# Attention scores on one core: the second score product over all 128 rows, with zeros in place of the other head

## The chip, the cores and the metric

The kernel runs on one core of a Trainium2 chip. Its engines have queues of their own and meet only at semaphores: TensorE (PE, with the weight loads shown apart as PEld), VectorE (DVE), ScalarE (ACT), GpSimd (POOL) and SyncE (SP, which issues most DMAs). The metric is device time of one execution in microseconds (us), lower is better.

## The reference, cut to what matters

Two kinds of transformer block follow each other, two layers of each, on 512 tokens of width 1024. Both have an attention with heads of 64 features. In the first kind it is grouped: eight query heads share two key heads, and every token sees every other.

```python
proj = rms_norm(x, attn_norm_g[i]) @ w_in[i]
q, k, v, u, vv = jnp.split(proj, split_at, axis=-1)
q = axial_rope(rms_norm(q.reshape(b, s, N_HEADS, HEAD_DIM), q_norm_g[i]), tables)
k = axial_rope(rms_norm(k.reshape(b, s, N_KV_HEADS, HEAD_DIM), k_norm_g[i]), tables)
attn_o = gqa_attention(q, k, v)
```

In the second kind the attention is causal and dilated, with four heads, beside a convolution and a gated delta rule. All is float32, and the feed-forward halves of the blocks hold most of the products.

## The kernel before, in words

Activations lie feature-major: 128 features on the partitions, 512 tokens along the free axis. Products run in float32r, which holds fewer bits, so an operand is split into a high and a low part, and a dense product is made of three: high by high, high by low and low by high (`mm3`, L307 to L309).

A chunk of the attention holds two heads of 64 features, one on partitions 0 to 63 and one on 64 to 127 (`UP`, `DN`). For the scores the three products are folded into two. `stack_q` makes one tile a head: the high part of the query on the head's own partitions and its low part on the other 64. `stack_k` makes one tile a head with the high part of the key on both halves, so that one product over 128 rows gives high by high plus low by high. The third term, high by low, is a second product into the same PSUM tile. Its operands are the head's own 64 rows of the query tile and of a tile with the low parts of both heads (`kl` in the first kind of block, `akl` in the second).

A unit is 128 queries of one chunk, both heads: two pairs of products (L654 and L655, in the second kind of block L1285 and L1286), for each head the row maximum (DVE, L657), the exponential with its sum (ACT, L659), then a transposition of the result by four products (L547), a copy out of PSUM (ACT for one head, L668, DVE for the other, L670), and the products with the values (L676). There are 16 units in a layer of the first kind, with 512 keys each. A layer of the second kind has 8 units, with 256, 256, 384 and 512 keys (L1288 to L1313 are their later steps).

`Driver` sets the order of the instructions once, when the program is written. It keeps a clock of assumed durations, and puts the short chains (the units among them) in front of a background of dense products. On the chip each engine works through its queue in that order and waits where an operand is late. Two units may be in flight (`st.flight < 2`), so their score products often stand together, eight in a row, with the transpositions behind them.

Squares for the norms go through a ring of two buffers called `nsq` (pool `K.np`), in `Norm.feed`, `Post.add` and once in `consts2`. POOL sums them up (L525) and later makes the reciprocal root (L453).

Of the kernel before, what the change touches and what calls it, by code (L numbers as in the profile page):

```python
# [9 lines left out]
F32 = mybir.dt.float32  # L10
# [3 lines left out]
ALU = mybir.AluOpType  # L14
# [11 lines left out]

# columns of the per-feature parameter array
C1 = {}
# [29 lines left out]

# ---- order of emission: a foreground of short chains over a background of dense products
class Driver:  # L60
# [93 lines left out]
def tl(K, tag, bufs, dt=F32, n=512, pool=None):  # L154
    """working tile of the phase's pool"""
    return (pool or K.pool).tile([128, n], dt, tag=tag, bufs=bufs, name=_nm(K, tag))


def x_slot(K, k, nm="x"):
    """the slot of a residual chunk; the residual itself waits in DRAM while others use it"""  # L160
    return K.xp.tile([128, 512], F32, tag=f"x{k}", name=_nm(K, nm))
# [37 lines left out]

# ---- weights: one stream for the whole kernel, loaded ahead, split into two exact float32r parts  # L200
IN1 = [10, 6, 11, 7, 12, 8, 13, 9, 4, 5, 0, 1, 2, 3]
AQ, AK, AV, CV, CG, GQ, GK, GV, GG = 0, 2, 4, 6, 8, 10, 14, 18, 22
# projections of the second block in the order they are made: delta rule (two heads), convolution, attention, gate
ORDER2 = ("d0", "c0", "c1", "d1", "a0", "g0", "g1", "a1", "g2", "g3")


# mixed chunks in the order they are ready
KORDER2 = (2, 3, 4, 5, 6, 7, 0, 1)
# [55 lines left out]
def w_ahead(K, upto, fine=False):  # L264
    """loads and splits up to (not with) number upto, as far as there is room"""
    nc = K.nc
# [52 lines left out]
def thin_job(K, src, H, post):  # L319
    """32 output rows: both parts of the weights in one stationary operand, their rows summed later"""  # L320
    def g():
        ps = ps_d(K)
        w, _ = next_w(K, src)
        parts = job_parts(H)
        for p in parts:
            for k in range(KD):
                wk = w[:, k * 64:k * 64 + 64]
                K.nc.tensor.matmul(ps[:64, p], wk, H.hi[k][:, p], start=(k == 0), stop=False)
                K.nc.tensor.matmul(ps[:64, p], wk, H.lo[k][:, p], start=False, stop=(k == KD - 1))
                if k == 1:  # L330
                    w_ahead(K, K.wpos + 1)
                yield 2 * MM / len(parts)
        done_w(K)
        post(ps[:64, :])

    K.drv.job(g())
# [39 lines left out]
def last_pair(K, src, xh, xl, order, post):  # L376
    """output chunks 6 and 7; the last products go by halves of the tokens, so that what waits for
    one half runs beside the products of the other"""
    n = len(order)
# [31 lines left out]
def split_into(K, hi, lo, src, act=True):  # L411
    """exact hi + lo parts of a float32 tile"""
    nc = K.nc
    if act:
        nc.scalar.copy(out=hi, in_=src)
    else:
        nc.gpsimd.tensor_scalar(hi, src, 1.0, 0.0, ALU.mult, ALU.add)
    nc.vector.tensor_tensor(lo, src, hi.bitcast(F32), ALU.subtract)
# [5 lines left out]
def stack_q(K, sa, sb, src):  # L424
    """query operands of two heads: the high part on a head's own partitions, the low part on the others"""
    nc = K.nc
# [3 lines left out]


def stack_k(K, ka, kb, lo, src):
    """key operands of two heads: the high part on both halves, the low part on a head's own partitions"""
    nc = K.nc
    for s, own, other in ((ka, UP, DN), (kb, DN, UP)):
        nc.scalar.copy(out=s[own, :], in_=src[own, :])
        nc.scalar.copy(out=s[other, :], in_=src[own, :])
        nc.vector.tensor_tensor(lo[own, :], src[own, :], s[own, :].bitcast(F32), ALU.subtract)


def tok_sums(K, acc, n=4, tag="ts"):
    """[128 tok, n] sums over the features (of each half, for n = 8)"""
    v = tiny(K, n, tag)
# [13 lines left out]
def bcast_cols(K, r, sb=None):  # L457
    """[128 tok, 4] columns -> [128, 512], the same row on every partition"""
    nc = K.nc
# [9 lines left out]
def half_rsqrt(K, acc, hv, scale, tag):  # L469
    """sums over features and their scaled rsqrt for half of the tokens, the same row on every partition"""  # L470
    nc = K.nc
# [12 lines left out]
class Norm:  # L484
    """rms norm: the gain goes into the split operand, 1/rms is left for the products"""

# [7 lines left out]
    def feed_half(self, k, x, hv, sq):  # L494
        """one half of the tokens"""
        K, nc = self.K, self.K.nc
# [46 lines left out]
def tok_transpose(K, src):  # L543
    """feature-major [128 d, 512 t] -> psum [128 tok, 4, 128 d]"""
    ps = ps_m(K)
# [13 lines left out]
def block1_mix(K, i, H, F):  # L559
# [21 lines left out]
    st.attn_done = 0  # L581
    st.flight = 0

    def qk_post(gcol, extra, then):
        """head norm over sqrt(extra) and rotation; 1/rms of the token is folded into that of the head"""
        def post(ps):
# [28 lines left out]
    def k_then(rot):  # L615
        kk, lo = (tl(K, "ka", 1, F32R), tl(K, "kb", 1, F32R)), tl(K, "kl", 1, F32R)
        stack_k(K, *kk, lo, rot)

        def start():
            st.k = (kk, lo)  # L620
        return start
# [14 lines left out]
    def attn_chunk(c):  # L636
        def then(rot):
# [7 lines left out]
            def unit(qb):  # L645
                yield lambda: st.k is not None and st.v is not None and st.flight < 2
                st.flight += 1
                kk, klo = st.k
                qs = slice(qb * 128, (qb + 1) * 128)
                ps_ = []  # L650
                for j in range(2):
                    rows = slice(64 * j, 64 * j + 64)
                    ps = ps_m(K)
                    nc.tensor.matmul(ps, qq[j][:, qs], kk[j], start=True, stop=False)  # L654
                    nc.tensor.matmul(ps, qq[j][rows, qs], klo[rows, :], start=False, stop=True)  # L655
                    nm = tiny(K, 1, "nm")
# [221 lines left out]
def tanh_silu2(K, th, y):  # L878
    """2 * silu(y)"""
    nc = K.nc  # L880
# [4 lines left out]
def block2_mix(K, i, H):  # L885
# [19 lines left out]

    # ---- decay and write strength, one column a (block, head)
    nc.scalar.activation(out=K.ea[i], in_=K.adt[i][:, 0:4], func=AF.Exp)
# [4 lines left out]
    def ab_post(ps):  # L912
# [3 lines left out]
        def g():  # L916
# [14 lines left out]
            nc.vector.tensor_scalar(beta, beta, 0.5, 0.5, ALU.mult, ALU.add)  # L931
            # softplus(x) = max(x, 0) + log1p(e), e = exp(-|x|), log1p(e) = 2 atanh(e / (2 + e))
            nc.vector.tensor_scalar(na, ad, -1.0, None, ALU.mult)
# [52 lines left out]
    class Half:  # L986
        """two heads of the delta rule"""

# [79 lines left out]

        # within a chunk: A = q k^T o decay, T = (1 + M)^-1 by doubling the solved block size
        def intra(self, b):  # L1070
# [68 lines left out]

        # across chunks  # L1140
        def rec(self):
# [62 lines left out]
        def out(self, h):  # L1204
            """gate, back to feature-major, split"""
            m = 4 + 2 * self.hp + h
# [25 lines left out]

    # ---- dilated attention: the three patterns share one maximum, keys weighted by their count
    class Attn:
# [6 lines left out]
        def qk_post(self, which):  # L1241
            def post(ps):
# [8 lines left out]
                else:  # L1251
                    lo = tl(K, "akl", 1, F32R)
                    stack_k(K, *two, lo, a)
                    self.k = two, lo
            return post
# [18 lines left out]
        def unit(self, qb):  # L1274
            qq, (kk, klo) = self.q, self.k
            n = (qb + 1) * 128
# [5 lines left out]
            for j in range(2):  # L1282
                rows = slice(64 * j, 64 * j + 64)
                ps = ps_m(K)
                nc.tensor.matmul(ps[:, :nn], qq[j][:, qs], kk[j][:, :nn], start=True, stop=False)  # L1285
                nc.tensor.matmul(ps[:, :nn], qq[j][rows, qs], klo[rows, :nn], start=False, stop=True)  # L1286
                s = tl(K, "sc", 3)
# [46 lines left out]

    # ---- conformer convolution
    st.cg = [None, None]
# [129 lines left out]
class Post:  # L1466
    """x += rms_norm(y) * gain, then the next norm, by halves of the tokens"""

# [93 lines left out]
def build(ctx, tc, A, out, n1=2, n2=2):  # L1562
# [19 lines left out]
    def consts2():  # L1582
        """what only the second block needs"""
        msk = K.const.tile([128, 5, 128], U8, tag="msk", name="msk")
# [91 lines left out]
def _consts():  # L1676
    """arrays that depend on shapes alone"""
    f = np.float32
# [36 lines left out]
def _tiles(w):  # L1715
    """[L, K, N] -> [L, N / 128, 128, K] : for each 128 columns, k chunks side by side"""
    L, Kd, N = w.shape
# [4 lines left out]
def _cols(v):  # L1722
    """[L, n * 128] -> [L, 128, n]"""
    L = v.shape[0]
    return v.reshape(L, -1, 128).transpose(0, 2, 1)


def prepare(I):
    A = _consts()
    I = {k: np.asarray(v) for k, v in I.items()}  # L1730
    A["xT"] = np.ascontiguousarray(I["x"][0].T.reshape(8, 128, 512).transpose(1, 0, 2).reshape(128, 4096))
    # chunk c of the attention holds heads c and c + 4, which use key heads 0 and 1
    hp = np.concatenate([np.arange(64) + 64 * h for c in range(4) for h in (c, c + 4)])
# [49 lines left out]
```

## Time and profile before

| | |
|---|---|
| median of three runs | 2633.65 us (2633.11, 2633.65, 2636.53) |
| profiled execution | span 2636.6 us; the time shown that stands beside it is 2636.53, so next to nothing lies around the span |
| PE busy | 2560.8 us, 97% of the span, 12988 products |
| weight loads (PEld) | 2068.5 us, 78% |
| DVE, ACT, POOL busy | 1538.3 us (58%), 1032.3 us (39%), 516.8 us (20%) |
| granted TensorE clock, mean | 0.992 of full speed |

A record of PE covers its product from the start of its stream to the modelled end, and records overlap. The distance from one start to the next is therefore what a product costs. A load record shows when the stationary operand of the product was brought into the array. "<-issue" behind an idle time means that the profile shows nothing that the engine waited for.

### The profile page before, as it was taken

Reading aid. Unit: us, or ns where it says so; the run is one execution under the profiler, and the core shown is the slowest. Engines: PE = TensorE matmul, PEld = TensorE weight load, DVE = VectorE, ACT = ScalarE, POOL = GpSimd, SP = SyncE. Lnnn points to the kernel's source line nnn. Section 1 sums busy time; section 2 is a strip of 40 time slices with the busy share of each in tenths; the row PEclk is TensorE's granted clock in tenths of the full one; section 3 lists DMA queues with packets and bytes.
Section 4 is the critical chain, followed back from the end, with each engine's and each line's share of the span. In section 5 each row is a group of like instructions: output and inputs, shape, how many; then the busy total and the mean of one; then the engine's idle time right before and its main releaser. Section 6 shows DMA issues by size and latency. Waiting matters only on the chain. (4 is left out here: it accounts for less than half of the span.)

```text
span 2636.6 us, 33494 instructions
## 1 busy us (share of the span) xinstructions
PE 2560.8 (97%) x12988; PEld 2068.5 (78%) x12988; DVE 1538.3 (58%) x2380; ACT 1032.3 (39%) x1715; POOL 516.8 (20%) x457
## 2 busy tenths in 40 slices
PE   8999999999999999999999999999889999999998
PEld 6777888878777888877777888888877777888887
DVE  6667666336766666246897554432578875644323
ACT  5554433224544433234345442222343445422221
POOL 3322111002232111003120131110221310311101
PEclk9999999999999999999999999999999999999999
DMA  4113232332113323331111322333221113232232
GB/s 162 37 33 105 96 96 95 96 109 78 33 57 100 96 96 97 112 98 41 57 41 57 96 84 100 97 92 96 87 72 37 45 42 95 85 99 96 94 94 76
DMA packets 69854, 216.05 MB, mean 82 GB/s; under 512 B 8256, under 2 KB 11968, under 8 KB 69696
## 3 DMA queue, kind: packets, MB, share of 16 engines
q1 hardware_dynamic: 68336, 212.40, 25.3%
q8 instruction: 102, 1.67, 0.3%
q10 hardware_dynamic: 1360, 1.52, 0.2%
q14 instruction: 56, 0.46, 0.1%
HBM read 207.60 MB, written 6.29 MB: 81 GB/s over the span
## 5 line engine op out<-in xcount | busy, mean ns | idle before, releaser
L307 PE MATMUL pd<-hh,wh 128*128 128x512 f32 (+1 forms) x2064 | 801.1, 392 | 12.0 <-ACT wh L285 7.8
L308 PE MATMUL pd<-hl,wh 128*128 128x512 f32 (+1 forms) x2064 | 802.2, 390 | 6.7 <-DVE hl L517 4.1
L309 PE MATMUL pd<-hh,wl 128*128 128x512 f32 (+1 forms) x2064 | 797.1, 388 | 0.9 <-DVE wl L286 0.9
L285 ACT CAST wh<-wr 128x1024 fp32r<-128x1024 f32 (+2 forms) x407 | 400.8, 986 | 985.4 <-PE pd L308 942.8
L286 DVE TENSOR_TENSOR wl<-wr,wh 128x1024 fp32r<-128x1024 f32 (+2 forms) x407 | 472.8, 1163 | 403.7 <-ACT wh L285 388.9
L307 PEld LDWEIGHTS pd<-hh,wh 128*128 128x128 f32 x2064 | 388.1, 189 | 88.1 <-ACT wh L285 7.8
L308 PEld LDWEIGHTS pd<-hl,wh 128*128 128x128 f32 x2064 | 390.8, 189 | 83.6 <-DVE hl L517 7.2
L309 PEld LDWEIGHTS pd<-hh,wl 128*128 128x128 f32 x2064 | 389.7, 189 | 75.0 <-DVE wl L286 2.0
L309 PE MATMUL pd<-gh,wl 128*128 128x512 f32 (+1 forms) x704 | 269.0, 382 | 0.0
L308 PE MATMUL pd<-gl,wh 128*128 128x512 f32 (+1 forms) x704 | 269.0, 382 | 0.0
L307 PE MATMUL pd<-gh,wh 128*128 128x512 f32 (+1 forms) x704 | 268.9, 382 | 0.0
L308 PEld LDWEIGHTS pd<-gl,wh 128*128 128x128 f32 x704 | 132.6, 188 | 28.3
L309 PEld LDWEIGHTS pd<-gh,wl 128*128 128x128 f32 x704 | 132.6, 188 | 28.3
L307 PEld LDWEIGHTS pd<-gh,wh 128*128 128x128 f32 x704 | 132.6, 188 | 28.3
L1542 POOL TENSOR_TENSOR fz<-fz,nrB 128x512 f32<-128x512 f32 x44 | 77.6, 1763 | 365.6 <-ACT fz L1541 365.6
L856 POOL TENSOR_TENSOR fy<-fy,fy 128x512 f32<-128x512 f32 x44 | 56.8, 1290 | 383.1 <-DVE fy L850 367.4
L1549 DVE TENSOR_TENSOR fz<-pd,fz 128x512 f32<-128x512 f32 x42 | 29.1, 692 | 138.3 <-PE pd L309 135.4
L846 DVE TENSOR_TENSOR fh<-pd,nrB 128x512 f32<-128x512 f32 x88 | 60.5, 688 | 59.7 <-PE pd L309 54.7
L525 POOL TENSOR_TENSOR nacc<-nacc,nsq 128x512 f32<-128x512 f32 x30 | 46.2, 1541 | 240.3 <-ACT nsq L524 239.8
L1360 DVE SCALAR_TENSOR_TENSOR cz<-cy,dwh,cz 128x501 f32<-128x501 f32 (+21 forms) x120 | 89.3, 753 | 1.2 <-ACT cz L1358 0.3
L1540 DVE TENSOR_TENSOR fz<-pd,nrB 128x512 f32<-128x512 f32 x42 | 28.9, 691 | 102.6 <-PE pd L309 102.6
L848 ACT ACTIVATE fy<-fh,cols 128x512 f32<-128x512 f32 x88 | 71.9, 817 | 36.2 <-DVE fh L846 36.2
(399 smaller groups left out, 3551.4 us busy)
## 6 DMA issues: line engine op xcount, KB each, us to landing
wr<-in_w_up_dram SPq DMA_DIRECT2D x132, 512.0 KB, 3.4
wr<-in_w_in_dram SPq DMA_DIRECT2D x80, 512.0 KB, 3.3
wr<-in_w_down_dram SPq DMA_DIRECT2D x64, 512.0 KB, 3.5
wr<-in_w_gate_dram SPq DMA_DIRECT2D x44, 512.0 KB, 3.3
wr<-in_w_down_dram SPq DMA_DIRECT2D x32, 384.0 KB, 3.1
wr<-in_w_o_dram SPq DMA_DIRECT2D x32, 256.0 KB, 2.8
wr<-in_w_out_dram SPq DMA_DIRECT2D x16, 512.0 KB, 3.3
xd<-x SPq DMA_DIRECT2D x16, 256.0 KB, 2.0
```

The source lines that it names most:

```text
L285: nc.scalar.copy(out=hi[:, cs], in_=raw[:, cs])
L286: nc.vector.tensor_tensor(lo[:, cs], raw[:, cs], hi[:, cs].bitcast(F32), ALU.subtract)
L307: nc.tensor.matmul(ps, wh, xhi, start=start, stop=False)
L308: nc.tensor.matmul(ps, wh, xlo, start=False, stop=False)
L309: nc.tensor.matmul(ps, wl, xhi, start=False, stop=stop)
L525: (nc.vector if last else nc.gpsimd).tensor_tensor(self.acc, self.acc, sq, ALU.add)
L846: nc.vector.tensor_tensor(h, ps, F.rB, ALU.mult)
L848: nc.scalar.activation(out=y, in_=h, func=AF.Identity, scale=col("cw1", tt), bias=col("cb", tt))
L856: nc.gpsimd.tensor_tensor(y, y, part.pop(t), ALU.mult)
L1360: nc.vector.scalar_tensor_tensor(zt[:, s:], y[:, :S - s], w(30 - s), zt[:, s:], ALU.mult, ALU.add)
L1542: nc.gpsimd.tensor_tensor(z, z, F.rB, ALU.mult)
L1549: nc.vector.tensor_tensor(z, ps, z, ALU.mult)
```

## The change

Each head gets a low tile of its own, taken from the `nsq` ring when the mixer of a layer begins. POOL writes zeros to the 64 partitions of the other head (two memsets a layer), and `stack_k` puts the low part on the head's own 64. The second product then takes the whole query tile and the whole low tile: the extra rows multiply the low part of the query by zero. The number of columns stays. The tiles `kl` and `akl` are gone. Lines behind it move by some 8.

```diff
+def low_keys(K):
+    lo = tl(K, "nsq", 2, F32R, pool=K.np), tl(K, "nsq", 2, F32R, pool=K.np)
+    for t, other in zip(lo, (DN, UP)):
+        K.nc.gpsimd.memset(t[other, :].bitcast(F32), 0.0)
+    return lo
...
-    for s, own, other in ((ka, UP, DN), (kb, DN, UP)):
+    for s, l, own, other in ((ka, lo[0], UP, DN), (kb, lo[1], DN, UP)):
...
-        nc.vector.tensor_tensor(lo[own, :], src[own, :], s[own, :].bitcast(F32), ALU.subtract)
+        nc.vector.tensor_tensor(l[own, :], src[own, :], s[own, :].bitcast(F32), ALU.subtract)
...
-                    nc.tensor.matmul(ps, qq[j][rows, qs], klo[rows, :], start=False, stop=True)
+                    nc.tensor.matmul(ps, qq[j][:, qs], klo[j], start=False, stop=True)
...
-                nc.tensor.matmul(ps[:, :nn], qq[j][rows, qs], klo[rows, :nn], start=False, stop=True)
+                nc.tensor.matmul(ps[:, :nn], qq[j][:, qs], klo[j][:, :nn], start=False, stop=True)
```

TensorE's queue keeps its order throughout. At the start of the first attention it stands like this before (`ka` and `kb` are the high key tiles of the two heads, `qa` and `qb` the query tiles, `pm` the scores):

```order
L654 MATMUL pm_914<-ka_728,qa_891 128x512
L655 MATMUL pm_914<-kl_730,qa_891 128x512
L307 MATMUL pd_853<-hh_175,wh_795 128x512
L654 MATMUL pm_921<-kb_729,qb_892 128x512
L655 MATMUL pm_921<-kl_730,qb_892 128x512
```

and now like this, with two tiles of the `nsq` ring in place of `kl`, every row at its old place:

```order
L662 MATMUL pm_917<-ka_732,qa_894 128x512
L663 MATMUL pm_917<-nsq_224,qa_894 128x512
L307 MATMUL pd_856<-hh_175,wh_798 128x512
L662 MATMUL pm_924<-kb_733,qb_895 128x512
L663 MATMUL pm_924<-nsq_225,qb_895 128x512
```

Only POOL's queue gets more rows. At the start of the first layer, between the last sums of the input's norm and its reciprocal root (`normr`), it held:

```order
L525 TENSOR_TENSOR nacc_117<-nacc_117,nsq_158 128x512
L525 TENSOR_TENSOR nacc_117<-nacc_117,nsq_165 128x512
L525 TENSOR_TENSOR nacc_117<-nacc_117,nsq_172 128x512
L453 TENSOR_TENSOR normr_213<-normv_211,cst 128x4
L453 TENSOR_TENSOR vvr_316<-vvv_314,cst 128x8
```

and now holds:

```order
L533 TENSOR_TENSOR nacc_117<-nacc_117,nsq_158 128x512
L533 TENSOR_TENSOR nacc_117<-nacc_117,nsq_165 128x512
L533 TENSOR_TENSOR nacc_117<-nacc_117,nsq_172 128x512
L436 MEMSET nsq_224 64x512
L436 MEMSET nsq_225 64x512
L461 TENSOR_TENSOR normr_213<-normv_211,cst 128x4
L461 TENSOR_TENSOR vvr_320<-vvv_318,cst 128x8
```

The two memsets stand ahead of the reciprocal root, and the second and third layers look the same. In the fourth they stand among the sums of a norm that is made by halves of the tokens:

```order
L461 TENSOR_TENSOR postr_15121<-postv_15119,cst 128x2
L436 MEMSET nsq_15361 64x512
L518 TENSOR_TENSOR nacc_15199<-nacc_15199,py_14481 128x256
L436 MEMSET nsq_15362 64x512
L518 TENSOR_TENSOR nacc_15199<-nacc_15199,py_14571 128x256
L461 TENSOR_TENSOR postr_15178<-postv_15176,cst 128x2
```

Without the two memset rows this is the order before.

## Rows read from the trace of the kernel before

**Rows 1.** Windows over one attention stage of each kind, busy us (instructions), granted clock

```profile
95.00:190.00 95.00, 94.06 (x605) 66.41 (x604) 63.17 (x105) 54.91 (x128) 21.83 (x20) 0.96 0.07 22
...
1395.00:1465.00 70.00, 69.28 (x381) 49.69 (x379) 52.10 (x105) 37.81 (x90) 5.50 (x5) 0.98 0.20 62
```

**Rows 2.** Waits of PE from 95 to 190 us: total, times, longest

```profile
PE pm L654 <- DVE qb L429: 0.9, 1, 0.9
```

**Rows 3.** Timeline of PE, two dense products: start, duration

```profile
97.17 0.39 PE L308 MATMUL pd<-hl,wh 128*128 128x512 f32 x1
97.40 0.40 PE L309 MATMUL pd<-hh,wl 128*128 128x512 f32 x1
```

**Rows 4.** Timeline of the weight loads, the load for the second of these

```profile
97.18 0.19 PEld L309 LDWEIGHTS pd<-hh,wl 128*128 128x128 f32 x1
```

**Rows 5.** Timeline of PE, score products of a unit, then transpositions

```profile
148.47 0.51 PE L654 MATMUL pm<-ka,qa 128*128 128x512 f32 x1
148.91 0.49 PE L655 MATMUL pm<-kl,qa 64*128 64x512 f32 x1
149.33 0.50 PE L654 MATMUL pm<-kb,qb 128*128 128x512 f32 x1
...
150.18 0.66 PE L547 MATMUL pm<-cst,tmp 128*128 128x128 f32 x4
...
152.28 1.09 PE L547 MATMUL pm<-cst,p 128*128 128x128 f32 x8
```

**Rows 6.** Timeline of the weight loads there, with idle time before

```profile
149.33 0.19 PEld L654 LDWEIGHTS pm<-kb,qb 128*128 128x128 f32 x1 [0.24 <-issue]
```

**Rows 7.** Lines L655 and L1286: count, duration in ns, first and last start, shapes

```profile
L655 PE MATMUL pm<-kl,qa x32: 491/500/792, 98.0 to 751.3; 64*128 64x512 f32 x32
...
L1286 PE MATMUL pm<-akl,aqa x16: 380/410/502, 1398.6 to 2194.6; 64*128 64x256 f32 x8, 64*128 64x384 f32 x4, 64*128 64x512 f32 x4
```

**Rows 8.** Timeline of PE, score products of the second kind of block

```profile
1441.30 0.38 PE L1286 MATMUL pm<-akl,aqa 64*128 64x256 f32 x1
1441.61 0.38 PE L1285 MATMUL pm<-akb,aqb 128*128 128x256 f32 x1
```

**Rows 9.** Timeline of PE, dense products of 256 columns

```profile
1880.94 0.28 PE L307 MATMUL pd<-gh,wh 128*128 128x256 f32 x1
1881.05 0.28 PE L308 MATMUL pd<-gl,wh 128*128 128x256 f32 x1
1881.17 0.28 PE L309 MATMUL pd<-gh,wl 128*128 128x256 f32 x1
```

**Rows 10.** Timeline of PE, a burst: first product, next work, last transposition

```profile
158.36 0.49 PE L654 MATMUL pm<-ka,qa 128*128 128x512 f32 x1
...
161.80 0.51 PE L308 MATMUL pd<-ml,wh 128*128 128x512 f32 x1
...
164.15 0.60 PE L547 MATMUL pm<-cst,p 128*128 128x128 f32 x4
```

**Rows 11.** Timeline of ACT, the first and the last exponential of that burst

```profile
160.05 0.69 ACT L659 ACTIVATE p<-pm,nm 128x512 f32<-128x512 f32 x1 [1.32 <-DVE nm L657]
...
162.71 0.69 ACT L659 ACTIVATE p<-pm,nm 128x512 f32<-128x512 f32 x1
```

**Rows 12.** Timeline of ACT, exponentials of the burst at 148.47

```profile
151.07 0.69 ACT L659 ACTIVATE p<-pm,nm 128x512 f32<-128x512 f32 x1
...
154.92 0.69 ACT L659 ACTIVATE p<-pm,nm 128x512 f32<-128x512 f32 x1
```

**Rows 13.** Windows of low clock inside attention stages, first and last of five

```profile
100.95:107.78 6.83, 6.83 (x19) 4.63 (x19) 3.78 (x6) 3.03 (x10) 0.10 (x1) 0.50 0.05 17
...
1401.43:1404.85 3.42, 3.42 (x13) 2.11 (x12) 1.72 (x5) 0.60 (x2) 0.00 (x0) 0.50 0.00 0
```

**Rows 14.** Timeline of POOL, reciprocal root of the first layer, idle before

```profile
26.04 1.03 POOL L453 TENSOR_TENSOR normr<-normv,cst 128x4 f32<-128x4 f32 x1 [6.66 <-DVE normv L451]
```

**Rows 15.** Groups of POOL by line: count, busy us, mean ns

```profile
L417 POOL TENSOR_SCALAR gh<-fy 128x512 fp32r<-128x512 f32 x44 | 29.1, 661 | 3.9
```

More of the change, by code (lines that the diff above doesn't have):

```diff
@@ L582, in block1_mix @@
     st.flight = 0
+    klo = low_keys(K)
     def qk_post(gcol, extra, then):
@@ L615, in k_then @@
     def k_then(rot):
-        kk, lo = (tl(K, "ka", 1, F32R), tl(K, "kb", 1, F32R)), tl(K, "kl", 1, F32R)
-        stack_k(K, *kk, lo, rot)
+        kk = tl(K, "ka", 1, F32R), tl(K, "kb", 1, F32R)
+        stack_k(K, *kk, klo, rot)
         def start():
-            st.k = (kk, lo)
+            st.k = kk
         return start
@@ L647, in unit @@
                 st.flight += 1
-                kk, klo = st.k
+                kk = st.k
                 qs = slice(qb * 128, (qb + 1) * 128)
@@ L651, in unit @@
                 for j in range(2):
-                    rows = slice(64 * j, 64 * j + 64)
                     ps = ps_m(K)
                     nc.tensor.matmul(ps, qq[j][:, qs], kk[j], start=True, stop=False)
-                    nc.tensor.matmul(ps, qq[j][rows, qs], klo[rows, :], start=False, stop=True)
+                    nc.tensor.matmul(ps, qq[j][:, qs], klo[j], start=False, stop=True)
                     nm = tiny(K, 1, "nm")
@@ L1231, in g_post @@
         return post
+    klo = low_keys(K)
     class Attn:
@@ L1251, in post @@
                 else:
-                    lo = tl(K, "akl", 1, F32R)
-                    stack_k(K, *two, lo, a)
-                    self.k = two, lo
+                    stack_k(K, *two, klo, a)
+                    self.k = two
             return post
@@ L1274, in unit @@
         def unit(self, qb):
-            qq, (kk, klo) = self.q, self.k
+            qq, kk = self.q, self.k
             n = (qb + 1) * 128
@@ L1282, in unit @@
             for j in range(2):
-                rows = slice(64 * j, 64 * j + 64)
                 ps = ps_m(K)
                 nc.tensor.matmul(ps[:, :nn], qq[j][:, qs], kk[j][:, :nn], start=True, stop=False)
-                nc.tensor.matmul(ps[:, :nn], qq[j][rows, qs], klo[rows, :nn], start=False, stop=True)
+                nc.tensor.matmul(ps[:, :nn], qq[j][:, qs], klo[j][:, :nn], start=False, stop=True)
                 s = tl(K, "sc", 3)
```

## The prediction

> **What bounds the kernel now.** I read first the windows over the stages that the change touches, one attention of each kind [rows 1]; the other layer of each kind looks alike. PE is busy for 94.06 of 95 us in the one and 69.28 of 70 us in the other, DVE for 63.17 and 52.10, ACT for 54.91 and 37.81. So PE's queue sets the pace. The view of waits then says what PE waits for in the first: one operand, for 0.9 us [rows 2]. Time that PE gives up there shortens the kernel until another engine's result is late.
>
> But a busy PE is not a fast one, and the third view, the timeline, shows it. Two dense products of 512 columns start 0.23 us apart [rows 3], and the load for the second begins at 97.18, just behind the start of the first at 97.17: it lies under the stream [rows 4]. Among the score products the starts are 0.44 and 0.42 us apart, and the step out to the transpositions is as long (two products fill 149.33 to 150.18, 0.85 us) [rows 5]. The load there begins with its own product, after 0.24 us idle that no semaphore explains [rows 6]. What differs is the rows: the product before it runs over 64 rows, its neighbours over 128. Each passage from 128 rows to 64 or back costs about 0.43 in place of 0.23.
>
> **What the change does to PE.** It makes the second products 128 rows tall. A 64-row product of 512 columns has a record of 0.49 us, the 128-row one beside it 0.50 or 0.51 [rows 5], so columns set the stream, and twice the rows cost nothing. What goes is the passage: one into and one out of each second product.
>
> First kind of block: 32 second products for one head [rows 7] and 32 for the other, 128 passages of 0.43 - 0.23 = 0.20 us: 25.6 us. Second kind: 16 and 16 [rows 7], 64 passages. At 256 columns the passage takes 0.31 us [rows 8] where dense products stand 0.11 and 0.12 apart [rows 9], so 0.19 each: 12.2 us (the wider ones are taken alike). Gross 37.8 us.
>
> The load of a 128-row operand behind a 128-row score product is not in the trace in just this place. Its bounds are the dense step of 0.23 and the present 0.43. I take 0.23: in shape, type and columns the new product is the same as a dense one.
>
> The first section on packing (The mechanism) in the Trainium skill's page "TensorE: Matmul & The Clock Gate" says that a weight load overlaps products in flight only when its row group differs, or when it goes to a background buffer. By the first half of that rule a full-height load would wait wherever the one before is full-height, and the change would give 0 instead of 37.8 us. The dense rows, with a full-height load under a full-height stream, do not agree with that half.
>
> **What is given back.** The order is fixed, so the gain lasts only while the exponentials keep up. Score products mostly come in bursts of eight, 1.6 us shorter each by the count above. Two bursts show what they meet.
>
> The burst from 158.36 takes until 161.80, and its last transposition starts at 164.15 [rows 10], 5.79 us after the start. By PE alone it would start after 4.19. The four exponentials start at 160.05 to 162.71 [rows 11], 0.89 apart on average, 0.69 long. Their pace is ACT's: it equals that of the present pairs of products (0.86), and won't follow products at 0.46. The first moves up by one passage to 1.49 after the start, the last then ends near 1.49 + 3 x 0.89 + 0.69 = 4.85. The transposition comes there in place of 5.79: 0.94 of 1.6 us is kept.
>
> The burst from 148.47 is tighter. The second exponential ends at 151.07 + 0.69 = 151.76 [rows 12] and its transpositions start at 152.28 [rows 5], 0.5 us later. These are followed on ACT by the copy of their result and the next two exponentials, so they hold up the rest. Here about 0.5 of 1.6 us is kept.
>
> The two together keep 45% (1.46 of 3.2), and 25.6 becomes 11.5 us. The bounds: 30% (7.7) and all (25.6). For the second kind I have no such pair; its first exponentials work on fewer columns, so I take a value between 45% and all, 70%: 8.5 us, with bounds 5.5 and 12.2.
>
> **The clock.** In the attention stages PE's clock is granted at 0.50, the lower level of 1.2 GHz, in five stretches, the first 6.83 us, the last and the three between 3.4 us each [rows 13], 20.5 us together. Work that runs there at half speed loses half the time, 10.2 us. Ahead of them stood score products with their idle passages, at times together with a wait. With denser products I expect most of these stretches to go, and take three quarters of the loss, 7.7 us, between nothing and 10.2.
>
> **What costs nothing.** Eight memsets of 64x512 on POOL. The trace has no such memset. The nearest row is an element-wise pass over 128x512 at 0.66 us [rows 15]; from nothing to 0.66 each. In the first layer POOL idles 6.66 us ahead of the reciprocal root [rows 14], which waits for DVE. The second memset has to wait for the last reader of its buffer, but that is a sum on which the root depends as well, with transpositions, a DVE reduction and a small DVE instruction between. So the memsets lie under that chain. The second and third layers have the same order. In the fourth, the memsets stand between sums that wait for ACT. Were all this cover gone, eight times 0.66 is 5.3 us. The subtractions on DVE are as many as before, into two tiles. The `nsq` ring is next needed by sums of a later phase, which need the attention's output and so come after the last score product anyway. The DMA queues are untouched.
>
> **The sum.** 11.5 + 8.5 + 7.7 - 0 = 27.7 us. The profiled execution's 2636.6 us would become 2608.9. The median lies 3 us below it. If those runs have fewer low stretches, there is less clock to regain, which argues for a little less; but the 70% may be low. I take 27.7 off the median: 2606 us, 1.1% faster.
>
> **Rivals.** *Nothing is given back*: all 37.8 us and most of the 10.2 us, below 2596. For it: PE waits for one operand only in the stage [rows 2]. Against it: the margins of 0.5 us above. 6%.
>
> *ACT takes nearly everything*: less than 30% of the first kind and 45% of the second remain, and no clock, so 5.4 to 14 us, 2619 to 2628. For it: the present pace of 0.86 us for a pair is just that of the exponentials. Against it: ACT is busy for only 54.91 of 95 us [rows 1], so between bursts it catches up. 8%.
>
> *The change doesn't do what it says*: the passage is a matter of an accumulating second product rather than of its rows, and the new ones start 0.43 apart as before. The time stays at 2634. For it: every 64-row product here is also an accumulating one. Against it: L308 and L309 accumulate as well, at 0.23. 3%. The half rule on loads named above would give the same time, and shares this chance.
>
> *Slower, by the clock*: waits for exponentials leave PE idle in short pieces at each burst, and the clock falls to 0.50 for much of the attention. Each microsecond there loses half, so 55 us more at 1.2 GHz eat the whole 27.7, and 66 us make it 2639, slower by over 0.2%; the stages of [rows 1] and their like have 330 us. For it: the clock does fall in this stage [rows 13]. Against it: it now stays at 0.96 to 0.98 on average [rows 1] although every passage leaves PE half idle, and the new waits are fewer than the passages that go. 3%.
>
> **How the numbers follow.** The forecast has 80%. Its ends: 13.2 us gained (7.7 + 5.5, no clock) is 2620; 37.8 us, everything kept and no clock, is 2596. The range 2596 to 2620 leaves out the first rival, most of the second and the last two, some 18%. A measurement of this kernel can tell about 0.2%, 5.3 us, from no change. Faster by more than that: 80 + 6 + 8 = 94%; within: 3%; slower: 3%.
>
> **What would show it.** In the profile after: score products 0.23 us apart with their loads begun under the stream before; new waits of PE for the exponential (L659 before) at transpositions, 8 to 16 us in all; fewer low stretches in the attention stages; the stages 95 to 190 and its fellow shorter by some 8 to 10 us each, those of the second kind by 4 to 6; nothing else moved. I am wrong if the products stay at 0.43, if waits take over 25 us, or if POOL's root comes late.

## The result

The changed kernel takes 2601.6 us (2599.1 to 2604.1, four runs) against 2633.4 us before in the same session: the ratio is 0.9878, 95% interval 0.9866 to 0.9890. That is 31.8 us or 1.2% faster, inside the range of 2596 to 2620 and 4 us below the forecast of 2606.

The two profiled executions differ by more, 2636.6 against 2602.3 us of span. About 1.8 us lie around the span of the changed kernel (2604.12 for 2602.3). So the profiled execution before was probably slower than the three times shown for it, and not, as was read ahead of the prediction, the one of 2636.53.

### The profile page after: what moved, and what is told of

It reads as the page before. It is cut to its first block, busy times and chain, and to the rows that moved or that the text cites. A ratio compares the mean times of both kernels' runs of the same rounds, so it can differ in the third digit from the quotient of the medians.

```text
span 2602.3 us, 33506 instructions
## 1 busy us (share of the span) xinstructions
PE 2523.3 (97%) x12988; PEld 2061.3 (79%) x12988; DVE 1535.7 (59%) x2380; ACT 1027.9 (39%) x1715; POOL 518.0 (20%) x465
```

## The profile after

The windows over one attention stage of each kind answer to [rows 1]. The stages end 12 and 30 us earlier (the last product with the values starts at 174.9 in place of 186.6, and at 1433.3 in place of 1463.7; the 30 hold what the layers ahead had gained). The windows are drawn around them and are 10 and 4 us shorter; the stages themselves lost 12.1 and 6.7 us (table below). PE's clock is now granted in full in both:

```profile
95.00:180.00 85.00, 82.58 (x613) 65.57 (x612) 63.29 (x106) 54.30 (x129) 23.82 (x22) 1.00 0.08 28
...
1375.00:1441.00 66.00, 65.27 (x383) 50.12 (x382) 53.07 (x105) 39.32 (x91) 5.48 (x5) 1.00 0.22 72
```

The timeline of PE over the burst that began at 158.36 before [rows 10] (start, duration). Products stand 0.23 us apart after the first, whichever of the two they are, and the last transposition starts 4.39 us after the first product (154.93 - 150.54), 5.79 before:

```profile
150.54 0.50 PE L662 MATMUL pm<-ka,qa 128*128 128x512 f32 x1
150.87 0.39 PE L663 MATMUL pm<-nsq,qa 128*128 128x512 f32 x1
151.10 0.40 PE L662 MATMUL pm<-kb,qb 128*128 128x512 f32 x1
151.34 0.39 PE L663 MATMUL pm<-nsq,qb 128*128 128x512 f32 x1
...
154.93 0.60 PE L555 MATMUL pm<-cst,p 128*128 128x128 f32 x4
```

At 256 columns, in the second kind of block, the step is 0.12 us:

```profile
1374.80 0.28 PE L1294 MATMUL pm<-nsq,aqa 128*128 128x256 f32 x1
1374.92 0.28 PE L1293 MATMUL pm<-akb,aqb 128*128 128x256 f32 x1
```

The weight loads of the same stretch answer to [rows 6]. The load for the third product begins at 150.88, under the stream of the second. Farther on a load waits for an exponential:

```profile
150.88 0.19 PEld L662 LDWEIGHTS pm<-kb,qb 128*128 128x128 f32 x1
...
154.19 0.42 PEld L555 LDWEIGHTS pm<-cst,p 128*128 128x128 f32 x4 [0.21 <-ACT p L667]
```

The idle time ahead of the second products' loads is gone. Before, the waits of the weight loads in the first stage (95 to 190 us; total, times, longest) began with this row, and L663 has none after:

```profile
PEld pm L655 <- issue: 8.2, 32, 0.4
```

ACT there answers to [rows 11]: the four exponentials start 0.66 us apart, where they had started 0.89 apart:

```profile
152.03 0.69 ACT L667 ACTIVATE p<-pm,nm 128x512 f32<-128x512 f32 x1 [1.12 <-DVE nm L665]
...
152.71 0.68 ACT L667 ACTIVATE p<-pm,nm 128x512 f32<-128x512 f32 x1
...
153.37 0.69 ACT L667 ACTIVATE p<-pm,nm 128x512 f32<-128x512 f32 x1
...
154.03 0.69 ACT L667 ACTIVATE p<-pm,nm 128x512 f32<-128x512 f32 x1
```

What had set the old pace shows in DVE's timeline of the kernel before. Each maximum waited for PE:

```profile
160.25 0.69 DVE L657 TENSOR_REDUCE nm<-pm 128x1 f32<-128x512 f32 x1 [0.24 <-PE pm L655]
161.12 0.69 DVE L657 TENSOR_REDUCE nm<-pm 128x1 f32<-128x512 f32 x1 [0.17 <-PE pm L655]
```

The waits of the weight loads for exponentials grew, as was forecast. In the first stage before:

```profile
PEld pm L547 <- ACT p L659: 1.4, 6, 0.4
```

The same row of the kernel after (95 to 180 us):

```profile
PEld pm L555 <- ACT p L667: 4.4, 13, 1.0
```

In both layers together they come to 8.8 us in 26 waits, 2.3 us in 10 before; the forecast was 8 to 16 us.

POOL's timeline answers to [rows 14]. A memset takes 0.52 us; the second waits for DVE's sum. The root starts 2.5 us behind it, 0.13 us after DVE's result is there at 26.24 (0.08 us before the change):

```profile
23.33 0.52 POOL L436 MEMSET nsq<- 64x512 f32 x1 [3.09 <-DVE nacc L533]
26.37 1.03 POOL L461 TENSOR_TENSOR normr<-normv,cst 128x4 f32<-128x4 f32 x1 [2.53 <-issue]
```

For all comparisons below, a stage is the time from its first score product to its last product with the values, read off PE's timeline, in us. In brackets stands for how long PE's clock was granted at the lower level (0.50) in it.

| kernel | first kind, layer 1 | layer 2 | second kind, layer 1 | layer 2 |
|---|---|---|---|---|
| before | 89.0 (6.8) | 90.8 (10.2) | 65.4 (3.4) | 65.3 |
| memsets only | 86.0 | 87.5 (3.4) | 65.4 (3.4) | 65.3 |
| changed | 76.9 | 76.9 | 58.7 | 60.1 |
| first kind only | 77.0 | 76.9 | 65.4 (3.4) | 65.3 |
| second kind only | 89.0 (6.8) | 87.5 (3.4) | 58.7 | 60.1 |
| grouped | 78.6 | 78.5 | 61.1 | 62.5 |

## The experiments

All medians below stand beside the kernel before on the same chip in the same session. The edits are cut to the lines that matter.

**The change in one kind of block alone.** `klo` and the 128-row second product stand in the first kind, or in the second; the other kind keeps its lines. From the first of the two, against the changed kernel:

```diff
...
-                nc.tensor.matmul(ps[:, :nn], qq[j][:, qs], klo[j][:, :nn], start=False, stop=True)
+                rows = slice(64 * j, 64 * j + 64)
+                nc.tensor.matmul(ps[:, :nn], qq[j][rows, qs], klo[rows, :nn], start=False, stop=True)
```

> The change in the first kind of block alone; the second kind keeps its 64-row products. Passage theory (each step between a 64-row and a 128-row product costs 0.2 us, and only that goes): the two stages keep the 12.1 and 13.9 us that they gained in the profile of the changed kernel, so 24 to 27 us off, 2607 to 2610. Rival (half of the gain is the clock, which falls or holds by chance of where idle pieces lie): the low-clock stretches come back in the stages and the gain is 15 to 20 us, 2614 to 2618.

> The change in the second kind of block alone. Passage theory: 6.7 and 5.2 us gained as in the changed kernel, so 10 to 13 us off, 2621 to 2624, and together with the first kind alone the whole 32 to 34. Rival (an effect of the whole kernel, say of the shared ring or of where tiles lie, and not of the products): the two parts don't add up to the whole, by more than 5 us.

The first kind alone gave 2612.9 against 2632.8 us, ratio 0.9924 (0.9906 to 0.9943); the second 2620.2, ratio 0.9952 (0.9935 to 0.9969). That is 19.9 and 12.6 us, together 32.5, within the expected 32 to 34: the parts add up, and the table shows that each stage that was changed is as long as in the changed kernel, to 0.1 us. But 19.9 is not the 24 to 27 us that I expected. The table says why. The stages did shrink to 77 us, but the profiled execution before had 17 us of low clock in its two first-kind stages, where two others with the same products had 3.4 and 10.2. I had booked the luck of one execution as gain. The rival's 15 to 20 us hold the number but not its reason: no low clock came back in those stages.

**Grouped.** The kernel before with its products in another order, all of them computed:

```diff
+                sc = [ps_m(K), ps_m(K)]
+                for j in range(2):
+                    nc.tensor.matmul(sc[j], qq[j][:, qs], kk[j], start=True, stop=False)
                 for j in range(2):
                     rows = slice(64 * j, 64 * j + 64)
-                    ps = ps_m(K)
-                    nc.tensor.matmul(ps, qq[j][:, qs], kk[j], start=True, stop=False)
-                    nc.tensor.matmul(ps, qq[j][rows, qs], klo[rows, :], start=False, stop=True)
+                    nc.tensor.matmul(sc[j], qq[j][rows, qs], klo[rows, :], start=False, stop=True)
...
```

> The kernel before, with the products of a unit in another order: both 128-row products, then both 64-row products (one on the upper, one on the lower rows). All four are computed as before. Passage theory: two passages a unit in place of four, so half of the gross 37.5 us is saved, 19 us, plus up to 0.2 us a unit (10 us) if products on different rows run side by side, less some given back: 12 to 25 us off, 2608 to 2621, and in the profile the second 64-row product starts at most 0.23 us after the first. Rival (a 64-row product is slow in itself, because its own load can't begin early): starts stay 0.43 us apart, time 2630 to 2636.

It took 2608.4 us, ratio 0.9905 (0.9889 to 0.9921), 24 us faster without one row added, at the upper end of what was expected. The timeline of PE shows the two 64-row products at the same time:

```profile
141.87 0.40 PE L653 MATMUL pm<-kb,qb 128*128 128x512 f32 x1
142.20 0.50 PE L656 MATMUL pm<-kl,qa 64*128 64x512 f32 x1
142.20 0.50 PE L656 MATMUL pm<-kl,qb 64*128 64x512 f32 x1
142.63 0.66 PE L547 MATMUL pm<-cst,tmp 128*128 128x128 f32 x4
```

The step into the pair is 0.33 and the step out 0.43, and there is none between them, on other rows but of the same height. This falls in with a rule of the Trainium skill, page "TensorEngine Tiling (Array Packing)", section Key Properties: a change of the tiling mode, not of the tile alone, drains the engine.

**Memsets only.** The kernel before, with the eight memsets on ring tiles that nothing reads.

```diff
...
+    low_keys(K)
...
```

> The kernel before with the eight memsets on tiles of the shared ring that nothing reads; the products are as before. Passage theory: nothing gained or lost, 2631 to 2636. Rival (the memsets hold up the reciprocal root or the sums on POOL): later by up to eight times 0.52 us, 2637.

Ratio 1.0003 (0.9991 to 1.0016). They are hidden. In this run both memsets of the first layer end before DVE's last sum and don't wait for it, so the wait that the changed kernel has there was not tried alone; that it holds nothing up rests on the 0.13 us above. The profile also gives the stage before without low clock: 86.0 us.

**All four products over 64 rows,** which leaves out low query by high key.

```diff
-                    nc.tensor.matmul(ps, qq[j][:, qs], kk[j], start=True, stop=False)
+                    nc.tensor.matmul(ps, qq[j][rows, qs], kk[j][rows, :], start=True, stop=False)
...
```

> The kernel before with all four score products of a unit over a head's own 64 rows, in the old order (first head, first head, second head, second head). Left out: the product of the low query with the high key. Passage theory: what costs is the change of height, not 64 rows, so inside a burst of products there is none left; two products of one head start at most 0.23 us apart at 512 columns, the two heads may even run side by side as the grouped run showed, and one passage into and one out of a burst remain. A stage of the first kind takes 73 to 78 us in place of 86 without low clock, the whole 2595 to 2608. Rival (64-row products are slow because their loads can't be hidden under products on the same rows): starts of one head's two products stay 0.4 us apart, and the time is 2625 or more.

2599.5 us (two runs), ratio 0.9865 (0.9838 to 0.9892), as expected. The heads run side by side. The second product of a head starts 0.33 us after the first of a burst, as it does in the changed kernel (150.54 to 150.87 above); from there on the products of a head stand 0.23 to 0.24 us apart. The height is not what is dear. PE's timeline:

```profile
150.08 0.49 PE L654 MATMUL pm<-ka,qa 64*128 64x512 f32 x1
150.09 0.49 PE L654 MATMUL pm<-kb,qb 64*128 64x512 f32 x1
150.41 0.39 PE L655 MATMUL pm<-kl,qa 64*128 64x512 f32 x1
...
150.64 0.39 PE L654 MATMUL pm<-ka,qa 64*128 64x512 f32 x1
...
150.88 0.39 PE L655 MATMUL pm<-kl,qa 64*128 64x512 f32 x1
```

Its stages of the first kind take 76.8 us, no less than in the changed kernel, although four products there fill less of PE. So PE's products no longer set that stage alone.

**No wait for exponentials.** The transpositions read a constant table; the attention's weights are left out of the output.

```diff
-                    pt = tok_transpose(K, ps_[j])
+                    pt = tok_transpose(K, K.cos)
...
```

> The changed kernel, with the transpositions reading a constant table in place of the exponentials' result (which leaves the attention's weights out of its output); all exponentials still run. If what is given back is the wait of the transpositions for the exponentials, the first-kind stages get shorter by the 3 to 4 us that these loads wait for in each, from 76.9 to 73 to 74 us, and the gross count of 12.5 us a stage comes out against 86.0 before (85.96 in the memset run, where no clock was low). If it is given back elsewhere (the copies out of PSUM, DVE's queue), the stage stays at 76 to 77.

2599.0 us, ratio 0.9863 (0.9842 to 0.9883); the first stages stayed at 76.9 us. That speaks against my theory as I had put it, but doesn't refute it, since the order changed too: the transpositions now stood behind up to nine dense products. The weight loads' waits in the first stage fell for the exponentials (4.4 in the changed kernel) and rose for the next link, the copy out of PSUM on DVE (0.7 there):

```profile
PEld pm L684 <- DVE pT L678: 1.4, 3, 0.7
PEld pm L555 <- ACT p L667: 0.9, 4, 0.3
```

**A later split.** In the changed kernel the finished chunk is split some 4 us later.

```diff
                 nc.vector.tensor_tensor(stc.o, stc.o, pl, ALU.mult)
+                yield 436, 4000
                 merged_split(c, stc.o, col("aog", c))
...
```

> The changed kernel; in the first kind the split of a finished chunk (POOL mh, DVE ml, ACT square) is written some 4 us later, so that DVE's queue no longer has the 1.8 us pass of ml between the maxima of the burst that kept only 0.37 of 1.6 us. If that pass is why the burst keeps so little, its period shrinks from 9.5 to about 8.5 us and the stage by 1 to 2 us; the whole by 2 to 4, about 2598. If ACT's pace is why, nothing changes by over 0.5 us a stage.

In the changed kernel DVE's timeline in the burst of 141.02 (148.47 before) shows a pass of 1.84 us between the third and the fourth maximum, and then PE waits for the fourth exponential:

```profile
143.72 0.68 DVE L665 TENSOR_REDUCE nm<-pm 128x1 f32<-128x512 f32 x1
144.63 1.84 DVE L734 SCALAR_TENSOR_TENSOR ml<-ao,cols,mh 128x512 fp32r<-128x512 f32 x1 [0.23 <-POOL mh L733]
146.39 0.68 DVE L665 TENSOR_REDUCE nm<-pm 128x1 f32<-128x512 f32 x1
```

On PE's timeline the wait reads:

```profile
147.93 0.66 PE L555 MATMUL pm<-cst,p 128*128 128x128 f32 x4 [0.66 <-ACT p L667]
```

With the later split the maxima follow each other (two in one row), and the pass comes behind them, and is shorter:

```profile
142.73 1.28 DVE L665 TENSOR_REDUCE nm<-pm 128x1 f32<-128x512 f32 x2
...
144.52 1.08 DVE L735 SCALAR_TENSOR_TENSOR ml<-ao,cols,mh 128x512 fp32r<-128x512 f32 x1
```

The period of the burst fell from 9.52 to 8.53 us (140.16 to 148.69), the stage to 75.3 us. The loads' wait for exponentials in it fell from 4.4 us to

```profile
PEld pm L555 <- ACT p L667: 1.8, 8, 0.3
```

The time did not follow: 2603.0 us, where about 2598 was expected. Behind the stage (170 to 220 us) PE's side waited for the last chunk's sums and for weights (the changed kernel waits 2.3 and 1.1 us there, for other operands):

```profile
PEld pd L307 <- ACT wh L285: 3.8, 1, 3.8
PEld pm L470 <- POOL star L461: 1.1, 1, 1.1
```

**A later split, but for the last chunk.** The same, with the delay left out for the last of the four chunks of a layer (`if not last:`, with `last = st.attn_done == 3`), beside the changed kernel run again:

> As the run with the later split, but the last chunk of a layer is split at once, as in the changed kernel. If the 1.6 us a stage that the later split gained was lost behind the stage because the last chunk's split came late (it feeds the sums on which the output products wait), both stages stay near 75.3 us, what follows the stage returns to the changed kernel's pace, and the whole is 2 to 4 us below the changed kernel in the same call. If it was lost to something else, the weight stream say, the time equals the changed kernel's within 1 us.

> The changed kernel once more, for the comparison on the same chip: 2599 to 2604, stages of 76.9, 76.9, 58.7 and 60.1 us.

2597.97 us (2596.3 to 2598.8) against 2601.0 (2599.1 to 2603.4) and 2633.6 before, ratios 0.9861 (0.9844 to 0.9877) and 0.9874 (0.9859 to 0.9889). The stages are 75.3 us, the wait behind them is as in the changed kernel, and the 3.0 us agree with two stages of 1.6. The runs of the two don't overlap, by 0.3 us, though the intervals of the ratios do. This is the fastest version that computes everything.

**A longer planned distance.** `yield 870, 3300` in place of `870, 2475` behind the score products of the changed kernel.

> The changed kernel with the planned distance from score products to transpositions raised from 2475 to 3300 (first kind only), so that more dense products stand between. If PE waits for exponentials because the transpositions follow too closely, the loads' waits of 4.4 us in the first stage fall by half or more and each stage shrinks by 1 to 3 us: 2596 to 2600. If ACT and DVE are the pace of the whole stage, the waits only move and the time stays at 2600 to 2603, or dense products run out later and it gets longer.

2616.0 us, ratio 0.9927 (0.9909 to 0.9945), slower than the changed kernel by some 13 to 14 us. Stages of 88.5 and 87.7 us drew dense products in, each with 3.4 us of low clock, and at their end the chains had no cover left. PE's waits from 95 to 230 us:

```profile
PE pd L307 <- DVE tmp L827: 2.2, 1, 2.2
PE pm L470 <- POOL star L461: 2.1, 1, 2.1
PE pm L684 <- ACT pT L676: 1.9, 1, 1.9
```

The loads' waits for exponentials did get shorter (1.0 us in 95 to 190), and it didn't matter. The loss lies in the two layers of the first kind: counted by PE's products, the 3000th starts 7.2 us later than in the changed kernel and the 5000th 13.6 us, and behind that the distance stays within 1 us. How it divides among these waits, the clock and the order was not measured.

## Why the prediction was right, step by step

**The passage: right.** Steps of 0.43 us became 0.23 to 0.235, at 256 columns 0.31 became 0.12. Gross that is 128 x 0.195 + 64 x 0.19 = 37.1 us, where 37.8 was forecast. Full-height loads begin under a full-height score product (the load of 150.88 under the product begun at 150.87). The rule of the Trainium skill, page "TensorE: Matmul & The Clock Gate", section The mechanism, in its half on row groups, does not hold there either.

**What is given back: right in kind, too large in size.** Free of the clock, the stages of the first kind give 85.96 - 76.95 = 9.0 us twice (for layer 2 this takes its stage to be as long as that of layer 1, as it is to 0.1 us in the changed and the grouped kernel). The second kind gives 6.7 and 5.2. The 6.7 holds a stretch of low clock: where neither layer has one, layer 1 is the shorter by 1.4 us (58.7 and 60.1, grouped 61.1 and 62.5), while before, with 3.4 us of low clock, it took 65.4 against 65.3. So the stretch cost about 1.5, and the products gave 5.2 in each layer. 18.0 of 25.0 us is 72%, where I had 45%; 10.4 of 12.2 is 85%, where I had 70%. Products gave 28.4 us in place of 20.0.

The step of the forecast that was wrong is the pace of the exponentials. I read 0.89 us as ACT's own, because it equalled the pace of the products. It was the products' pace: the maxima waited for PE, and freed of that the exponentials follow at 0.66. With that the worked example would have been 1.49 + 3 x 0.66 + 0.69 = 4.16 for the last exponential's end, ahead of PE's own 4.19, and 1.6 us kept; 1.4 were. The tight burst kept 0.37 where I said 0.5, for another reason than I gave: DVE's queue, not ACT's (the later split). And it is one tight burst of seven. The others, first product to first product, kept 4.1 (the first, with low clock; 1.0 against the memset run, which has none there), 1.2, 1.3, 1.2, 1.4 and 1.0 us. Two bursts were too few to take a share from.

**The clock: right for the profiled pair, not for the medians.** All 20.5 us of low clock in the stages were gone. By the table they had cost 3.0, 4.8 and 1.5 us, some 9.4 together, for a forecast of 7.7. That they went holds beyond this pair: with the old products the two first-kind stages had 17.1, 10.2 and 3.4 us of low clock in three profiled executions (before, second kind only, memsets only), and with the new products none in any, the longer distance apart. Outside the stages the changed kernel's execution had more of it (32.6 us against 25.5), and 37.9 us gained in the stages ended as 34.3 of span. Between the medians it is 31.8 us, of which products make 28.4, which leaves about 3 for the clock. Executions of equal clock agree: at a mean granted clock of 0.995 eight executions before span 2628.4 to 2629.5 us, two of the changed kernel 2599.6 and 2600.6, 29 us apart. So the sum came out near in part by luck, by two errors against each other: some 8 us too little for the products, some 4 too much for the clock.

**Costs at nothing: right.** The memsets alone change nothing that can be measured, and the root follows DVE's result as closely as before to 0.05 us.

**The rivals.** That nothing is given back comes near in the second kind (1.8 of 12.2 us) and fails in the first. That ACT takes nearly everything is refuted by 0.66; by its own shares that rival ended at 13.2 us and not at 14. That the passage is a matter of accumulation is refuted by the grouped run, in which the same accumulating products cost less. A fall of the clock in the attention stages appeared only where dense work was moved (the longer distance).

**Left open.** Of the 7 us that the first kind gives back, 3 came home with the later split. For the rest I have the waits for exponentials and copies, and no run that takes them away with the order kept.

## What to carry to other kernels

A product of another height costs PE a step on the way in and on the way out, 0.2 us each here. Look for it as idle time of the weight loads "<-issue", and mend it with rows of zeros or by putting products of one height together. Before an engine's pace is called its own, look at what it waits for: an interval that equals the bottleneck's may be the bottleneck's. And take the clock out of the profiled stretch before booking a gain: one execution had 17 us of low clock in two stages in which another had 3.4.

## What the hardware showed unexpectedly

Two 64-row products on the upper and the lower rows, of 512 columns each, started at the same hundredth of a microsecond (142.20) in the grouped run and ended together. In the run over 64 rows the kernel puts both products of one head into PE's queue ahead of both of the other, and yet the second head's first product started at 150.09, 0.01 us behind the first head's first and ahead of its second (150.41).

A stretch of 3.4 us at 1.2 GHz cost about 1.6 us in a stage of the first kind (87.5 against 86.0) and about 1.5 in the second, where two layers of unequal length nearly hid it (65.4 with it, 65.3 without).

A pass of DVE of the same shape took 1.84 us in one place and 1.08 in another (L734 and L735). What differs is POOL. In the changed kernel its sum over 128x512 ran beside the pass for all of 1.29 us, with the later split for 0.53 us:

```profile
144.63 1.29 POOL L743 TENSOR_TENSOR acc_a<-acc_a,tmp 128x512 f32<-128x512 f32 x1
```

```profile
143.76 1.29 POOL L744 TENSOR_TENSOR acc_a<-acc_a,tmp 128x512 f32<-128x512 f32 x1 [0.16 <-ACT tmp L743]
```

In the changed kernel, the run with the later split and four others, this pass stands 96 times. Where POOL is idle it takes 0.74 to 0.76 us, and each microsecond beside POOL's work adds about 0.8. So the pass that held up the tight burst seems to have been long because POOL's sum began with it; no run moves that sum alone.
